# Output projection and second feed-forward matrix of a fused block in products of 512 columns instead of 256

## The chip, the cores and the metric

One core of a Trainium2 chip runs the whole program. Its engines are TensorE (PE; a matmul is a MATMUL and a LDWEIGHTS of its stationary operand, shown as PEld), VectorE (DVE), ScalarE (ACT), GpSimd (POOL) and SyncE (SP), which issues most transfers. The metric is device time in microseconds: 2568.1 us, the median of three runs (2564.01 to 2571.09).

## The reference

A block of a hybrid model on 1024 tokens of width 1024, in float32. Cut to what the change touches:

```python
h = _rms(x, norm_mix_g)
p_nsa, p_rwkv, p_gdn, p_gate = split(h @ w_in)
o_a, o_b, o_c = _nsa(p_nsa), _rwkv7(p_rwkv), _gdn(p_gdn)          # 1024 x 512 each
gate = sigmoid(p_gate.reshape(1024, 3, 1024))
merged = gate[:, 0] * (o_a @ w_branch[0]) + gate[:, 1] * (o_b @ w_branch[1]) + gate[:, 2] * (o_c @ w_branch[2])
x = x + merged @ w_out                                            # 1024 x 1024
h = _rms(x, norm_ffn_g)
x = x + square(relu(h @ w_ff1)) @ w_ff2                           # 1024 x 4096, 4096 x 1024
```

## The kernel before

**Split products.** Every large product is made of three: each float32 operand is split into a rounded part (`hi`, type float32r) and a rest (`lo`), and hi·hi, hi·lo and lo·hi are summed in PSUM. A weight tile therefore goes through `load_w` (L242): SP transfers it into `wraw`, ACT casts it into `whi` (L253), and the rest `wraw - whi` goes into `wlo` (L258), which VectorE and GpSimd share as the argument `div` says. With `(1, 2)` VectorE takes the first half of the tile's row blocks and GpSimd the second, with `(0, 1)` GpSimd takes all. `TRAW` is the number of `wraw` buffers, `TBUF` that of `whi` and of `wlo`, for the first and the second tail.

**The tail.** `tail(hf, ...)` computes everything behind the three mixers for 512 tokens; `hf` is 0 or 1, so it runs twice. Its stages:

1. Branch products. For each of three branches, four tiles `or` of the mixer's output (128 x 512 each) are loaded and split into `oh` and `ol` (`OBUF` buffers each). Then for each of eight column blocks: load a weight tile of 512 x 128, load the gate tile `gin` (ACT makes a tanh of it in place), 12 matmuls of 512 columns, and VectorE multiplies the sum in PSUM by the gate (L1470). From the second branch on GpSimd adds this to `ms` (L1472). The third branch's results are split into `mh` and `ml`.
2. Output projection, by `accum` (L1430). The stationary operand is a 128 x 128 piece of `mh` or `ml` (128 tokens), the moving one a piece of the weight tile. One call takes 256 output columns and all eight row blocks (two weight tiles of 512 x 256); for each of four token blocks `st` it makes 24 matmuls of 256 columns and one add to `acc` (L1442), a tile that already holds `x`. Four calls cover the 1024 columns.
3. Norm (`norm_T`): the rows of `acc` are normalised, transposed and split into `h2h` and `h2l`.
4. Feed-forward, in eight groups of four row blocks of 128. `up` makes one block: two weight tiles of 512 x 128, 24 matmuls of 512 columns with the weight tile as stationary operand, then relu (ACT), square (VectorE) and the split into `fh` and `fl`. After the four (in the first group five) `up` of a group, four calls of `accum` bring the group's share of the second matrix into `acc`: each has one weight tile of 512 x 256, four token blocks, 12 matmuls of 256 columns and an add. So a group is 96 matmuls of 512 columns and 192 of 256.
5. Four writes of `acc` to `out` (L1519).

**What sets the order.** The first tail is a job that is stepped through beside the second half of the sparse attention (`nsa`, whose PSUM tiles are called `mps`, the tails' `fps`): `run` (L166) takes a piece of the tail whenever a share of PE's modelled time is owed to it, a piece being what lies between two `yield`. When the attention is done the rest of the first tail follows, then the second tail. The tile framework's scheduler, with a model of the times, then orders the instructions of each engine, and within an engine they run in that order. While the attention runs, two PSUM buffers serve the tail; afterwards there are six (`pst`, L1569).

## Time and profile before

| | |
|---|---|
| median of three runs | 2568.1 us (2564.01 to 2571.09) |
| the profiled execution | 2570.32 us, span 2568.6 us |
| mean granted PE clock | 0.964 |
| PE busy | 2414.0 us, 94% |
| DVE, ACT, POOL busy | 1488.7, 1044.3, 989.9 us |
| DMA | 217.05 MB, mean 84 GB/s |

The span runs from the first to the last instruction; the 1.7 us around it belong to the execution's time. Matmuls are pipelined, so the busy times of neighbours overlap: what a matmul occupies PE for is the distance from its start to the next one's start. Rows of several like instructions are merged (`x4`), with one duration for all. A few matmul records are missing from a trace. In the brackets of a timeline row stands the engine's idle time before it and who ended it.

### The profile page before, as it was taken

How to read it: one execution, taken by the hardware profiler on the slowest of the kernel's cores; microseconds unless marked ns; L12 is line 12 of the kernel's file. 1: busy time of each engine (PE TensorE's matmuls, PEld its weight loads, DVE VectorE, ACT ScalarE, POOL GpSimd, SP SyncE). 2: the span in 40 equal slices, each digit the busy share in tenths (PEclk: the TensorE clock that was granted, in tenths of full speed). 3: DMA queues.
4: the chain of work that ended last, by engine and by line, in shares of the span. 5: the costliest groups of instructions: out<-in, count | busy, mean ns of one | idle time of the engine just before them, and what ended most of it. 6: DMA issues, size and time to landing. Idle time of an engine off the chain costs nothing.

```text
span 2568.6 us, 41137 instructions
## 1 busy us (share of the span) xinstructions
PE 2414.0 (94%) x15509; PEld 2013.4 (78%) x15509; DVE 1488.7 (58%) x3325; ACT 1044.3 (41%) x2085; POOL 989.9 (39%) x975
## 2 busy tenths in 40 slices
PE   7989899999898999989999999899999999999999
PEld 4767676777777777777887778788888878899988
DVE  4587877673576666223557787764454444545444
ACT  5333423332343333225667675753322333423232
POOL 4444433333322121234446675343332345223332
PEclk9889889999999999999999999899999999999999
DMA  4222222222223122362214331025322354223233
GB/s 135 66 54 66 57 52 66 70 55 79 67 66 83 40 54 76 114 137 76 61 50 141 101 102 37 20 72 154 95 91 86 104 160 132 78 87 107 83 104 102
DMA packets 340214, 217.05 MB, mean 84 GB/s; under 512 B 78486, under 2 KB 314144, under 8 KB 340016
## 3 DMA queue, kind: packets, MB, share of 16 engines
q1 hardware_dynamic: 329152, 195.63, 27.2%
q10 hardware_dynamic: 9792, 17.83, 1.9%
q8 instruction: 122, 2.00, 0.3%
q0 software_dynamic: 1072, 0.96, 0.2%
q14 instruction: 76, 0.62, 0.1%
HBM read 178.16 MB, written 36.22 MB: 83 GB/s over the span
## 4 chain that ended last, share of the span: by engine, by line
PE 71%; DVE 15%; DMA 6%; ACT 4%; issue 2%; POOL 1%; SPq 0%; ACTq 0%; DVEq 0%; POOLq 0%
PE fps L96 53%; PE mps L96 15%; PE mps L100 3%; DVE inv_p L335 2%; DVE inv_u L337 1%; DMA gin<-gates 1%; DVE BK L549 1%; DVE gacc L881 1%; DMA cw<-in_nsa_cmp_w_dram 1%; DMA lb<-inv 1%; ACT P L1348 1%; DMA inv<-LT 1%; DVE ast L1343 1%; DVE PL L1391 1%; DVE AG L536 1%
## 5 line engine op out<-in xcount | busy, mean ns | idle before, releaser
L258 POOL TENSOR_TENSOR wlo<-wraw,whi 128x512 fp32r<-128x512 f32 (+2 forms) x408 | 528.6, 1297 | 940.1 <-ACT whi L253 907.4
L253 ACT CAST whi<-wraw 128x512 fp32r<-128x512 f32 (+1 forms) x408 | 286.2, 703 | 699.5 <-PE fps L96 612.0
L96 PE MATMUL fps<-hTh,whi 128*128 128x512 f32 x1024 | 448.7, 440 | 6.7 <-ACT rraw L423 3.5
L96 PE MATMUL fps<-hTh,wlo 128*128 128x512 f32 x1024 | 416.4, 411 | 3.4 <-POOL wlo L258 3.4
L96 PE MATMUL fps<-hTl,whi 128*128 128x512 f32 x1024 | 418.1, 410 | 0.0
L96 PE MATMUL fps<-wlo,fh 128*128 128x256 f32 x1024 | 266.6, 284 | 7.0 <-DVE wlo L258 7.0
L96 PE MATMUL fps<-whi,fl 128*128 128x256 f32 x1024 | 266.7, 283 | 0.0
L96 PE MATMUL fps<-whi,fh 128*128 128x256 f32 x1024 | 266.0, 284 | 0.6
L258 DVE TENSOR_TENSOR wlo<-wraw,whi 128x256 fp32r<-128x256 f32 (+1 forms) x207 | 142.2, 690 | 180.2 <-ACT whi L253 180.1
L96 PEld LDWEIGHTS fps<-hTh,wlo 128*128 128x128 f32 x1024 | 200.7, 196 | 50.8 <-POOL wlo L258 5.2
L96 PEld LDWEIGHTS fps<-hTh,whi 128*128 128x128 f32 x1024 | 201.4, 197 | 49.0 <-ACT whi L253 3.8
L96 PEld LDWEIGHTS fps<-hTl,whi 128*128 128x128 f32 x1024 | 202.4, 198 | 32.5
L1442 DVE TENSOR_TENSOR acc<-fps,acc 128x256 f32<-128x256 f32 x288 | 118.6, 422 | 178.5 <-PE fps L96 178.1
L96 PE MATMUL fps<-h2h,whi 128*128 128x512 f32 x512 | 200.1, 391 | 0.9 <-DVE h2l L290 0.9
L96 PE MATMUL fps<-h2h,wlo 128*128 128x512 f32 x512 | 200.0, 391 | 0.2 <-DVE wlo L258 0.2
L96 PE MATMUL fps<-h2l,whi 128*128 128x512 f32 x512 | 199.8, 390 | 0.0
L1362 POOL TENSOR_SCALAR P<-P,ast 128x64 f32<-128x64 f32 (+5 forms) x128 | 138.6, 1100 | 144.7 <-DVE ast L1355 112.6
L96 PEld LDWEIGHTS fps<-wlo,fh 128*128 128x128 f32 x1024 | 186.3, 192 | 8.8 <-DVE wlo L258 8.4
L96 PEld LDWEIGHTS fps<-whi,fh 128*128 128x128 f32 x1024 | 186.9, 192 | 3.8 <-ACT whi L253 2.2
L96 PEld LDWEIGHTS fps<-whi,fl 128*128 128x128 f32 x1024 | 187.4, 192 | 0.1
L1348 ACT ACTIVATE P<-mps,ast 128x128 f32<-128x128 f32 (+4 forms) x256 | 125.1, 494 | 80.5 <-DVE ast L1346 47.3
L1343 DVE TENSOR_REDUCE ast<-mps 128x1 f32<-128x128 f32 (+4 forms) x256 | 109.0, 441 | 49.5 <-PE mps L96 47.3
(465 smaller groups left out, 4946.4 us busy)
## 6 DMA issues: line engine op xcount, KB each, us to landing
wraw<-in_w_in_dram SPq DMA_DIRECT2D x152, 256.0 KB, 2.9
wraw<-in_w_ff_dram SPq DMA_DIRECT2D x128, 256.0 KB, 2.9
wraw<-in_w_ff_dram SPq DMA_DIRECT2D x64, 512.0 KB, 3.4
gates<-fst ACTq DMA_DIRECT2D x48, 256.0 KB, 2.0
wraw<-in_w_branch_dram SPq DMA_DIRECT2D x48, 256.0 KB, 3.0
gin<-gates SPq DMA_DIRECT2D x48, 256.0 KB, 3.0
wraw<-in_w_out_dram SPq DMA_DIRECT2D x16, 512.0 KB, 3.6
nsa_in<-fst ACTq DMA_DIRECT2D x20, 256.0 KB, 2.1
```

The costliest lines, as they stand in the source:

```text
L96: return self.note(self.nc.tensor.matmul(out, lhsT=lhsT, rhs=rhs, **kw))
L100: return self.note(self.nc.tensor.transpose(out, x, ident))
L253: nc.scalar.copy(hi, raw)
L258: eng.tensor_tensor(out=lo[:, x], in0=raw[:, x], in1=hi[:, x].bitcast(F32), op=OP.subtract)
L335: nc.vector.tensor_tensor(out=v, in0=lt[:n, s, None, s + 1:].to_broadcast([n, w, w]), in1=u[:n, s + 1:, s + 1:].rearrange("p t c -> p c t" ...
L337: nc.vector.tensor_reduce(out=u[:n, s, s + 1:], in_=v, axis=AX, op=OP.add)
L536: stt(out=ag[o, :, :, h], in0=ch2(sg)[o, :, c2], scalar=-1.0, in1=ch2(kk)[o, :, c2], op0=OP.mult, op1=OP.mult)
L549: tt(out=BK[HH[h], :, :, 1 - (x ^ h)], in0=ch2(t)[HH[h]], in1=ch2(WI)[HH[h]], op=OP.mult)
L1343: nc.vector.tensor_reduce(out=(mx if i == 0 else mx2)[:, b:b + 1], in_=ps[:, :n], axis=AX, op=OP.max, negate=True)
L1348: nc.scalar.activation(out=Pt[:, c:c + n], in_=tiles[i][:, :n], func=AF.Exp, bias=mx[:, b:b + 1], accum_out=(sm if i == 0 else sm2)[:, b:b ...
L1362: eng.tensor_scalar(out=Pt[:, c:c + n], in0=Pt[:, c:c + n], scalar1=r[:, b:b + 1], scalar2=None, op0=OP.mult)
L1442: tt(out=acc[:, st, c0:c0 + 256], in0=ps, in1=acc[:, st, c0:c0 + 256], op=OP.add)
```

## The change

`accum` takes 512 output columns and four row blocks in one call, instead of 256 columns and all row blocks (eight in the output projection). Its weight tiles are two row blocks by 512 columns, two of them to a call; they have as many bytes as the old ones of four by 256. A token block's sum is 12 matmuls of 512 columns and one add of 512. The output projection calls it for two column halves and two halves of the row blocks, a feed-forward group for two column halves. `yield` now stands behind each three matmuls of 512 columns instead of each six of 256.

The buffers: `whi` and `wlo` have three in the first tail and four in the second, not two; `oh` and `ol` four, not five; `or` and `gin`, which had two each, share three; `fh` and `fl` five in the first tail, not six.

```diff
--- before.py
+++ after.py
@@ -42,11 +42,12 @@
 TDIV = ((0, 1), (1, 2))
 FDIV = (0, 1)
 TRAW = (2, 2)
-TBUF = (2, 2)
+TBUF = (3, 4)
 FSPLIT = (1, 1)
 FRAW = 2
 FBUF = 2
-OBUF = 5
+OBUF = 4
+FBUFS = (5, 6)
 POOLB = (0, 2)
 KVBUF = 2
 SABUF = 5
@@ -1418,8 +1419,8 @@
 
         div = lambda: TDIV[hf] if self.tasks else TDIV[1]
 
-        def load(src, cols):
-            return self.load_w(src, 4, cols, wp, wbufs, TRAW[hf], div())
+        def load(src, kt, cols):
+            return self.load_w(src, kt, cols, wp, wbufs, TRAW[hf], div())
 
         with pool("tacc") as ap, pool("tw") as wp:
             acc = ap.tile([P, 4, D], F32, name="acc")
@@ -1427,19 +1428,18 @@
                 nc.sync.dma_start(out=acc[:, st], in_=a["x"][0, T.start + st * P:T.start + (st + 1) * P, :])
 
 
-            def accum(lhs, w_rows, kt, c0):
-                ws = [load(w_rows[j * 512:(j + 1) * 512, c0:c0 + 256], 256) for j in range(kt // 4)]
+            def accum(lhs, w_rows, k0, c0):
+                ws = [load(w_rows[(k0 + j) * P:(k0 + j + 2) * P, c0:c0 + 512], 2, 512) for j in (0, 2)]
                 for st in range(4):
                     m = slice(st * P, (st + 1) * P)
-                    ps = psum()[:, 0:256]
-                    for k in range(kt):
-                        (wh, wl), j = ws[k // 4], k % 4
-                        self.te.matmul(ps, lhsT=lhs[0](k)[:, m], rhs=wh[:, j, :], start=(k == 0), stop=False)
-                        self.te.matmul(ps, lhsT=lhs[0](k)[:, m], rhs=wl[:, j, :], start=False, stop=False)
-                        self.te.matmul(ps, lhsT=lhs[1](k)[:, m], rhs=wh[:, j, :], start=False, stop=(k == kt - 1))
-                        if k % 2:
-                            yield
-                    tt(out=acc[:, st, c0:c0 + 256], in0=ps, in1=acc[:, st, c0:c0 + 256], op=OP.add)
+                    ps = psum()
+                    for k in range(4):
+                        (wh, wl), j = ws[k // 2], k % 2
+                        self.te.matmul(ps, lhsT=lhs[0](k0 + k)[:, m], rhs=wh[:, j, :], start=(k == 0), stop=False)
+                        self.te.matmul(ps, lhsT=lhs[0](k0 + k)[:, m], rhs=wl[:, j, :], start=False, stop=False)
+                        self.te.matmul(ps, lhsT=lhs[1](k0 + k)[:, m], rhs=wh[:, j, :], start=False, stop=(k == 3))
+                        yield
+                    tt(out=acc[:, st, c0:c0 + 512], in0=ps, in1=acc[:, st, c0:c0 + 512], op=OP.add)
 
             with pool("tm") as mp:
                 mt = lambda n, dt=F32R, bufs=KT: mp.tile([P, 512], dt, name=n, tag="m" + n[-1], bufs=bufs)
@@ -1448,7 +1448,7 @@
                     for b in range(3):
                         oh, ol = [], []
                         for k in range(4):
-                            raw = op.tile([P, 512], F32, name="or", tag="or", bufs=2)
+                            raw = op.tile([P, 512], F32, name="or", tag="gin", bufs=3)
                             nc.sync.dma_start(out=raw, in_=self.o_spill["abc"[b]][k, :, T])
                             hi = op.tile([P, 512], F32R, name="oh", tag="oh", bufs=OBUF)
                             lo = op.tile([P, 512], F32R, name="ol", tag="ol", bufs=OBUF)
@@ -1456,8 +1456,8 @@
                             oh.append(hi)
                             ol.append(lo)
                         for dt in range(KT):
-                            wh, wl = load(a["w_branch"][0, b][:, dt * P:(dt + 1) * P], P)
-                            g = op.tile([P, 512], F32, name="gin", tag="gin", bufs=2)
+                            wh, wl = load(a["w_branch"][0, b][:, dt * P:(dt + 1) * P], 4, P)
+                            g = op.tile([P, 512], F32, name="gin", tag="gin", bufs=3)
                             nc.sync.dma_start(out=g, in_=self.gates[b * KT + dt, :, T])
                             nc.scalar.activation(out=g, in_=g, func=AF.Tanh, scale=0.5)
                             ps = psum()
@@ -1476,8 +1476,9 @@
                                 nc.scalar.activation(out=mh[dt], in_=m[dt], func=AF.Copy, scale=0.5)
                                 stt(out=ml[dt], in0=m[dt], scalar=0.5, in1=mh[dt].bitcast(F32), op0=OP.mult, op1=OP.subtract)
                 lhs = tuple((lambda k, t=t: t[k]) for t in (mh, ml))
-                for c0 in range(0, D, 256):
-                    yield from accum(lhs, a["w_out"][0], KT, c0)
+                for c0 in range(0, D, 512):
+                    for k0 in range(0, KT, 4):
+                        yield from accum(lhs, a["w_out"][0], k0, c0)
 
             with pool("th") as hp:
                 h2 = tuple(hp.tile([P, KT, 512], F32R, name=n) for n in ("h2h", "h2l"))
@@ -1490,15 +1491,15 @@
                     def up(ft):
                         ps = psum()
                         for kh in range(2):
-                            wh, wl = load(a["w_ff1"][0][kh * 512:kh * 512 + 512, ft * P:(ft + 1) * P], P)
+                            wh, wl = load(a["w_ff1"][0][kh * 512:kh * 512 + 512, ft * P:(ft + 1) * P], 4, P)
                             for j in range(4):
                                 k = kh * 4 + j
                                 self.te.matmul(ps, lhsT=wh[:, j], rhs=h2[0][:, k], start=(k == 0), stop=False)
                                 self.te.matmul(ps, lhsT=wh[:, j], rhs=h2[1][:, k], start=False, stop=False)
                                 self.te.matmul(ps, lhsT=wl[:, j], rhs=h2[0][:, k], start=False, stop=(k == KT - 1))
                                 yield
-                        hi = fp.tile([P, 512], F32R, name="fh", tag="fh", bufs=6)
-                        lo = fp.tile([P, 512], F32R, name="fl", tag="fl", bufs=6)
+                        hi = fp.tile([P, 512], F32R, name="fh", tag="fh", bufs=FBUFS[hf])
+                        lo = fp.tile([P, 512], F32R, name="fl", tag="fl", bufs=FBUFS[hf])
                         r = fp.tile([P, 512], F32, name="fr", tag="fr", bufs=2)
                         nc.scalar.activation(out=r, in_=ps, func=AF.Relu)
                         tt(out=r, in0=r, in1=r, op=OP.mult)
@@ -1511,8 +1512,8 @@
                             yield from up(ft)
                         now, fs = fs[:G], fs[G:]
                         lhs = (lambda k: now[k][0], lambda k: now[k][1])
-                        for c0 in range(0, D, 256):
-                            yield from accum(lhs, a["w_ff2"][0][g * P:(g + G) * P, :], G, c0)
+                        for c0 in range(0, D, 512):
+                            yield from accum(lhs, a["w_ff2"][0][g * P:(g + G) * P, :], 0, c0)
             self.summed = True
             yield
             for st in range(4):
```

On PE, the first tail's feed-forward behind the attention, before: the end of a group's first two `accum` calls and the start of the third. `whi_18043` and `whi_18169` are the weight tiles of the first and third call, `fps_18174` to `fps_18216` the four token blocks' sums of the third.

```order
L96 MATMUL fps_18048<-whi_18043,fh_17988 128x256
L96 MATMUL fps_18048<-wlo_18044,fh_17988 128x256
L96 MATMUL fps_18048<-whi_18043,fl_17989 128x256
L96 MATMUL fps_18174<-whi_18169,fh_17598 128x256
L96 MATMUL fps_18188<-whi_18169,fh_17598 128x256
L96 MATMUL fps_18202<-whi_18169,fh_17598 128x256
L96 MATMUL fps_18216<-whi_18169,fh_17598 128x256
L96 MATMUL fps_18188<-wlo_18170,fh_17598 128x256
```

Now, the same group's end of the first call and the second half of the second. `whi_17627` and `whi_17634` are the first call's two weight tiles, `whi_17704` is the second tile of the second call; `fps_17639` is the first call's first sum, `fps_17765` the next `up`.

```order
L97 MATMUL fps_17639<-whi_17627,fl_17481 128x512
L97 MATMUL fps_17639<-whi_17634,fh_17526 128x512
L97 MATMUL fps_17639<-wlo_17635,fh_17526 128x512
L97 MATMUL fps_17639<-whi_17634,fl_17527 128x512
L97 MATMUL fps_17639<-whi_17634,fh_17572 128x512
L97 MATMUL fps_17639<-wlo_17635,fh_17572 128x512
L97 MATMUL fps_17639<-whi_17634,fl_17573 128x512
L97 MATMUL fps_17709<-whi_17704,fh_17526 128x512
L97 MATMUL fps_17737<-whi_17704,fh_17526 128x512
L97 MATMUL fps_17723<-whi_17704,fh_17526 128x512
L97 MATMUL fps_17751<-whi_17704,fh_17526 128x512
L97 MATMUL fps_17765<-h2h_15819,whi_17768 128x512
```

A call's first sum is put off until the others of its call are done, in both orders. Before, the third weight tile is wanted directly behind the last product with the first one; now the fourth tile is wanted seven products behind the last product with the first.

On SP, the joint of the two tails, before: `w_ff` is the first tail's last group, `out_dram` its result, `gin` and `w_branch` belong to the second tail.

```order
L245 DMA wraw<-in_w_ff_dram 128x4x128 x6
L245 DMA wraw<-in_w_ff_dram 128x4x256 x4
L1519 DMA out_dram<-acc 128x1024
L1461 DMA gin<-gates 128x512
L245 DMA wraw<-in_w_branch_dram 128x4x128
L1519 DMA out_dram<-acc 128x1024
L1461 DMA gin<-gates 128x512
L245 DMA wraw<-in_w_branch_dram 128x4x128
L1519 DMA out_dram<-acc 128x1024
L1461 DMA gin<-gates 128x512
```

And now:

```order
L246 DMA wraw<-in_w_ff_dram 128x4x128 x6
L246 DMA wraw<-in_w_ff_dram 128x2x512 x4
L1452 DMA or<-o_a 128x512 x3
L1520 DMA out_dram<-acc 128x1024 x4
L1452 DMA or<-o_a 128x512
L1461 DMA gin<-gates 128x512 x5
L246 DMA wraw<-in_w_branch_dram 128x4x128
L1461 DMA gin<-gates 128x512
L246 DMA wraw<-in_w_branch_dram 128x4x128
L1461 DMA gin<-gates 128x512 x2
```

The first branch's tiles `or` have moved from well before the last group to either side of the four writes, which stand together, and five gate tiles follow before the next weight tile.

## Rows read from the trace of the kernel before

**Rows 1.** The page: busy time by engine; chain by line, shares of the span.
```profile
PE 2414.0 (94%) x15509; PEld 2013.4 (78%) x15509; DVE 1488.7 (58%) x3325; ACT 1044.3 (41%) x2085; POOL 989.9 (39%) x975
...
PE fps L96 53%; PE mps L96 15%; PE mps L100 3%; DVE inv_p L335 2%; DVE inv_u L337 1%; DMA gin<-gates 1%; DVE BK L549 1%; DVE gacc L881 1%; DMA cw<-in_nsa_cmp_w_dram 1%; DMA lb<-inv 1%; ACT P L1348 1%; DMA inv<-LT 1%; DVE ast L1343 1%; DVE PL L1391 1%; DVE AG L536 1%
```

**Rows 2.** Chain of waits, 1500 us to the end: start us, us, what.
```profile
1784.58 1.59 DVE wlo L258
...
2087.28 3.40 DMA gin<-gates
...
2205.17 359.31 PE fps L96 x2304
```

**Rows 3.** Stretches: us; PE, PEld, DVE, ACT, POOL busy (instructions); PE clock; DMA share; GB/s.
```profile
1400.00:1500.00 100.00, 94.17 (x550) 76.02 (x548) 75.48 (x166) 67.37 (x175) 71.25 (x57) 1.00 0.31 95
2205.00:2568.60 363.60, 359.46 (x2306) 328.50 (x2304) 172.95 (x292) 107.77 (x162) 113.83 (x94) 1.00 0.31 96
```

**Rows 4.** PE by time, second tail: start us, us, line, out<-in.
```profile
2232.55 0.64 PE L96 MATMUL fps<-whi,fh 128*128 128x256 f32 x4
...
2255.58 0.40 PE L96 MATMUL fps<-h2h,whi 128*128 128x512 f32 x1
...
2277.36 0.64 PE L96 MATMUL fps<-whi,fh 128*128 128x256 f32 x4
```

**Rows 5.** All engines by time, first tail: a group's bounds, and inside.
```profile
1819.18 0.64 PE L96 MATMUL fps<-whi,fh 128*128 128x256 f32 x4
...
1829.86 2.09 ACT L253 CAST whi<-wraw 128x1024 fp32r<-128x1024 f32 x2 [5.56 <-PE fps L96]
...
1830.96 0.74 PE L96 MATMUL fps<-whi,fh 128*128 128x256 f32 x4
1830.99 2.97 POOL L258 TENSOR_TENSOR wlo<-wraw,whi 128x512 fp32r<-128x512 f32 x2 [7.89 <-ACT whi L253]
1831.24 3.27 DVE L258 TENSOR_TENSOR wlo<-wraw,whi 128x512 fp32r<-128x512 f32 x2
1832.87 0.61 PE L96 MATMUL fps<-wlo,fh 128*128 128x256 f32 x3 [1.16 <-DVE wlo L258]
...
1865.82 0.64 PE L96 MATMUL fps<-whi,fh 128*128 128x256 f32 x4
```

**Rows 6.** Groups by shape, 2100 to 2560 us: busy us, mean ns.
```profile
L258 POOL TENSOR_TENSOR wlo<-wraw,whi 128x512 fp32r<-128x512 f32 x40 | 70.9, 1775 | 112.7 <-ACT whi L253 112.6
L1442 DVE TENSOR_TENSOR acc<-fps,acc 128x256 f32<-128x256 f32 x140 | 58.0, 422 | 90.1 <-PE fps L96 90.1
L253 ACT CAST whi<-wraw 128x1024 fp32r<-128x1024 f32 x40 | 41.9, 1048 | 90.4 <-PE fps L96 83.7 <-DMA wraw<-in_w_ff_dram 4.6 <-DMA wraw<-in_w_out_dram 2.1
L258 DVE TENSOR_TENSOR wlo<-wraw,whi 128x512 fp32r<-128x512 f32 x40 | 30.4, 759 | 37.5 <-ACT whi L253 37.5
L1472 POOL TENSOR_TENSOR ms<-ms,gin 128x512 f32<-128x512 f32 x16 | 24.1, 1507 | 5.8 <-DVE gin L1470 2.9 <-PE fps L96 2.6
L1470 DVE SCALAR_TENSOR_TENSOR gin<-gin,fps 128x512 f32<-128x512 f32 x14 | 9.6, 683 | 13.1 <-ACT gin L1462 11.4 <-PE fps L96 1.7
L1462 ACT ACTIVATE gin<-gin 128x512 f32<-128x512 f32 x14 | 8.8, 631 | 16.5 <-DMA gin<-gates 14.9 <-DVE wlo L258 1.6
```

**Rows 7.** DMA issues, from the page: KB each, median us to landing.
```profile
wraw<-in_w_ff_dram SPq DMA_DIRECT2D x64, 512.0 KB, 3.4
gin<-gates SPq DMA_DIRECT2D x48, 256.0 KB, 3.0
```

**Rows 8.** PE by time: last group of the first tail, first product of w_out.
```profile
2046.91 0.64 PE L96 MATMUL fps<-whi,fh 128*128 128x256 f32 x4
...
2146.88 0.66 PE L96 MATMUL fps<-whi,mh 128*128 128x256 f32 x4
```

**Rows 9.** Waits of PE beside the attention, 1383 to 1742 us: total, times.
```profile
PE mps L96 <- ACT P L1348: 7.5, 9, 1.7
PE mps L96 <- DVE PL L1391: 5.5, 5, 2.3
```

## The prediction

> **What bounds the kernel now.** I read the page's first and fourth parts, then the chain of waits in order of time, then the busy table by stretch, and last TensorE's own timeline where the chain lies on it. PE is busy for 94% of the span, and its products at L96 are 53% (the tails' and projections', `fps`) and 15% (`mps`) of the chain [rows 1]. In order of time the last 800 us are nearly all PE: in the first tail long pieces of it, parted by six pieces of 1.59 us of DVE writing `wlo`; one piece of 359.31 us in the second tail; and only around 2087 us a handful of waits for the gate tiles `gin` [rows 2]. The granted clock is 1.00 there and in the stretch where the first tail runs beside the attention, and PE is busy for 94 of 100 us even in that one [rows 3]. So a product that takes less of PE's time shortens the kernel nearly one for one, and everything else counts only where PE waits for it.
>
> **What a product costs.** Busy time is no price: matmuls overlap, so I take the distance between starts. In the second tail a group is 96 products of 512 columns (`up`) and 192 of 256 (`accum`). The 192 run from 2232.55 to 2255.58, 23.03 us, 0.1199 each; the 96 from 2255.58 to 2277.36, 21.78 us, 0.2269 each [rows 4]. Two of 256 cost 0.2399, one of 512 costs 0.2269: 13.0 ns less for the same columns. (256 more columns cost 107.0 ns, so 12.9 ns of either are a fixed part; 107.0 ns is one column a cycle at 2.4 GHz, the level of the granted clock of 1.00.) The changed kernel has half as many weight loads and half as many such parts. Products of 256 columns per tail: `accum` for the output projection 4 x 4 x 24 = 384, for the second feed-forward matrix 8 x 192 = 1536; both tails 3840, which become 1920 of 512. 1920 x 13.0 ns = 25.0 us. Of it 10.0 are in the second tail's groups (768 pairs), 2.5 in its output projection (192), 9.2 in the first tail's groups behind the attention (709), and 3.3 beside the attention (251).
>
> The Trainium skill (TensorE: Matmul & The Clock Gate, "Back-to-back issue gap") speaks against this: there a warm product of N columns takes N / 2.4 GHz plus 2.5 ns, so a pair would save 2.5 ns and the term would be 4.8 us. The rows have 13 ns at both widths, so the trace does not agree, and I go by it.
>
> **The wait inside the first tail's groups.** A group of the first tail lasts longer than one of the second: 1819.18 to 1865.82 is 46.64 us against 2232.55 to 2277.36, 44.81: 1.83 us more, with the same instructions [rows 4, 5]. Where it goes: at 1830.96 PE has issued four products with the third load's `whi` and stands until 1832.87; ACT's cast of that load began at 1829.86, when the buffer came free, GpSimd began its half at 1830.99, VectorE its half at 1831.24 behind an add to `acc`, and beside GpSimd it needed 1.59 us [rows 2, 5] where its mean for that tile is 0.76 [rows 6]. With two buffers the third load can't be split before an earlier one is used up. The chain shows this six times, so 6 x 1.83 = 11.0 us hang on it.
>
> In the changed order the place looks like this, counted from the end of the last `up` of a group with PE at 0.2269 a product. The sum that starts first is set aside after one product and finished late, so the first load's last reader is the 66th product. It starts at 65 x 0.2269 = 14.7 us and takes 0.40 [rows 4]; the fourth load waits for that, its cast takes 1.05 [rows 6], and `whi` is there at 16.2. PE needs it as the 73rd product, at 16.3. VectorE's half (0.76 to 1.59) is needed six products later, at 17.7, GpSimd's (1.78) twenty later, at 20.9. What is late next is thus the cast, by 0 to 0.3 us with the hand-overs. The first three loads are ahead: their transfers take 3.4 us [rows 7], two may be under way, and a step of 48 products now lasts 10.9 us instead of 5.8. I take 0.3 a group: 11.0 - 1.8 = 9.2 us gained. Bounds: all 11.0, or nothing if the old loss stays. The second tail has no such loss now, and with four buffers each load of a step has its own; nothing there.
>
> **The second tail's branch products.** From the last 256-column group of the first tail (2046.91) to the first product of the output projection (2146.88) are 99.97 us [rows 4, 8]. They hold 192 products of 256 and 3 x 8 x 12 = 288 of 512: 23.03 + 65.35 = 88.4 us. 11.6 us are lost, and the chain shows mostly transfers of `gin`. A `gin` buffer is held for the transfer 3.0 [rows 7], the tanh and the product (0.63 and 0.68) and, from the second branch on, GpSimd's add, 1.51 [rows 6]: 5.8 us. Two buffers give one product column block each 2.9 us, PE wants one each 2.72 (12 x 0.2269); three give 1.9. Against that, the raw tiles `or` now take turns in the same three buffers and `oh`/`ol` have four, not five: at each change of branch the third raw tile waits for the last `gin` of the branch before, 0.68 + 1.51 after its last product, then come 3.0 of transfer [rows 7] and some 0.6 each of cast and split (the tanh of that shape takes 0.63 [rows 6]), 6.4 in all, while PE has 24 products (5.4 us) on the first two: 1 to 3 us lost, twice. At the joint of the tails the four writes of `out` now stand ahead of all gate loads in SP's queue, and of the fourth `or`. PE has 36 products (8.2 us) before it needs that tile, which comes 0.68 (add) + 3.0 + 1.2 = 4.9 us, four issues and some hand-overs after the last product: 0 to 1.5 us. The seventh weight tile stands behind five gate loads, the last of which waits for the second product block: 0 to 1.5. Together 2 to 9 us where 11.6 are lost now. I take the upper end, 2.5 gained, as the ring of three has more takers; bounds from 9.6 gained to 10 lost, for no row shows this ring.
>
> **Small things.** An add to `acc` of 512 columns isn't in the trace; the nearest row is the product out of PSUM of that shape, 0.68 us against 0.42 for the add of 256 [rows 6]; below it can't fall under 0.42, above not beyond two of those. Three of these end a stretch that PE waits for (the norm of each tail, the last write): 3 x 0.26 = 0.8 us lost. The others lie beside products. The output projection's adds double in columns (16 x 0.26 = 4.2 us more of VectorE in each tail). In the second tail PE covers them. In the first they meet the attention, where PE stood for 13 us behind ACT's `P` and VectorE's `PL` [rows 9].
>
> **Beside the attention.** The order places the attention's last products deeper in the tail's work (behind the first group and into the next four `up`, no longer two thirds into the first group), in smaller pieces. No row of the kernel before shows what this order waits for. Below: the pieces fill the 13 us that PE stood, and a little more where it was free; 15 gained. Above: the finer alternation doubles the 13 and VectorE's 4.2 come on top; 20 lost, rounded up. PE is busy there for 94 of 100 us, so I take 0, beyond the 3.3 us of the rate.
>
> **Sum.** 25.0 + 9.2 + 2.5 - 0.8 = 35.9 us less. The profiled execution took 2570.3 us (span 2568.6); 2534.4. The median shown is 2568.1, 2.2 lower; so 2532. Its own range, with each term near its value: 2520 to 2546.
>
> **Rivals.** (a) The fixed part doesn't halve: the 512-column rows have another stationary operand (a weight tile, not `fh`), and if with `fh` the fixed part grew with the columns, nothing would come of the 25.0: 9.2 + 2.5 - 0.8 = 10.9 less, 2557. Against it, `up` and `accum` show the same 13 ns in the same stretch [rows 4]. With the 2.5 ns of the Trainium skill's page for a pair it would be 2552. (b) The alternation beside the attention costs the 20 us bounded above: 2552. For it speaks that the attention's chain goes through VectorE and ACT; against it the 94%. (c) It gains 15: 2517. (d) Slower than before: a step now needs two whole loads before it can end, and the second becomes the bound. If the second load's transfer too waited for the buffer, 3.4 + 1.05 + 1.80 = 6.3 us would stand against 2.7 us of work (12 products), 3.6 lost in each of the first tail's 20 steps, 72 us: 2604. It decides from 36 / 20 = 1.8 us a step. Two raw tiles ahead and four open sums in the order speak against it. That nothing changes would need two of these together.
>
> **Chances.** Forecast 0.63, (a) 0.06, (b) 0.15, (c) 0.10, (d) 0.06. 2508 to 2558 leaves out (d) and little else. What a measurement can tell from no change is 0.3%, 7.7 us: (b) lies 16 us below the median and (a) 11, with some 0.04 of both inside the bound. Faster 0.90, same 0.04, slower 0.06.
>
> **What would show it.** Right: in the second tail 192 products of 512 in 43.6 us a group without idle time; in the first, groups of 43.6 to 44.2 with no 1.6 us wait for `wlo`; 1920 pairs' worth of LDWEIGHTS gone; branch products of the second tail ending 65.4 + 9 us after the last group. Wrong: products of 512 with `fh` as stationary operand more than 0.235 apart; a wait for `whi` or `wlo` once a step; PE idle beyond 40 us beside the attention.

## The result, and the profile after

The changed kernel takes 2528.95 us (median of 4 runs, 2524.64 to 2535.23), the one before, run beside it, 2566.06 (4 runs, 2561.18 to 2571.09): ratio 0.9857, 95% interval 0.9827 to 0.9887, 37.1 us less. The forecast was 2532. The profiled execution took 2527.64 us, span 2525.9, mean granted PE clock 0.965.

The page of the changed kernel, busy time by engine, and two groups of costly instructions (busy us, mean ns). It answers to [rows 1, 6]:

```profile
PE 2377.5 (94%) x13589; PEld 1907.6 (76%) x13589; DVE 1472.0 (58%) x3197; ACT 1043.1 (41%) x2083; POOL 986.8 (39%) x975
...
L97 PE MATMUL fps<-whi,fl 128*128 128x512 f32 x512 | 191.0, 389 | 0.0
...
L1442 DVE TENSOR_TENSOR acc<-fps,acc 128x512 f32<-128x512 f32 x160 | 106.7, 686 | 101.4 <-PE fps L97 101.0
```

The 1920 matmuls and as many weight loads are gone (15509 to 13589), the share of PE is the same 94%, and the add of 512 columns, which no row of before had, takes 0.69 us (0.68 had been taken).

PE by time in the second tail (start us, us, what): first product of a group's `accum`, first `up`, next group. It answers to [rows 4]:

```profile
2200.12 0.39 PE L97 MATMUL fps<-whi,fh 128*128 128x512 f32 x1
...
2221.88 0.39 PE L97 MATMUL fps<-h2h,whi 128*128 128x512 f32 x1
...
2243.64 0.39 PE L97 MATMUL fps<-whi,fh 128*128 128x512 f32 x1
```

96 products of `accum` take 21.76 us, 96 of `up` 21.76: 0.2267 each, whichever the stationary operand. A group is 43.52 us, where it was 44.81.

The same in the first tail, two groups' starts, with the start of the second group and of the last one; it answers to [rows 5, 8]:

```profile
1755.56 0.62 PE L97 MATMUL fps<-whi,fh 128*128 128x512 f32 x2
...
1842.60 1.07 PE L97 MATMUL fps<-whi,fh 128*128 128x512 f32 x4
...
1886.12 1.07 PE L97 MATMUL fps<-whi,fh 128*128 128x512 f32 x4
...
2011.24 1.07 PE L97 MATMUL fps<-whi,fh 128*128 128x512 f32 x4
```

Here too a group is 43.52 us, to the hundredth what it is in the second tail. It was 46.64: the wait for `wlo` is gone.

The chain of waits from 1500 us on, its long pieces (start us, us, what), against [rows 2]:

```profile
1741.21 291.29 PE fps L97 x1284
...
2053.01 4.94 DMA wraw<-in_w_branch_dram
...
2061.97 4.19 DMA or<-o_b
2067.33 3.52 DMA gin<-gates
...
2085.51 3.85 DMA or<-o_c
...
2172.74 348.51 PE fps L97 x1536
```

What was PE parted by six pieces of `wlo` is one piece of 291 us. In the second tail's branch stage, though, the chain, which ran mostly through `gin`, now runs through the weight tiles `wraw` and the raw tiles `or`. PE at the change to the third branch, and its first product of the output projection:

```profile
2090.05 2.07 PE L97 MATMUL fps<-oh,whi 128*128 128x512 f32 x4 [5.29 <-ACT oh L254]
...
2114.85 1.20 PE L97 MATMUL fps<-whi,mh 128*128 128x512 f32 x4
```

and the windows around it (us; busy by engine; PE clock; DMA share; GB/s):

```profile
2085.00:2090.00 5.00, 0.00 (x0) 0.00 (x0) 2.56 (x4) 2.49 (x4) 4.26 (x5) 0.80 0.78 230
2090.00:2095.00 5.00, 4.95 (x12) 3.90 (x13) 2.50 (x4) 2.11 (x4) 3.42 (x5) 0.51 0.81 243
2095.00:2100.00 5.00, 5.00 (x24) 4.13 (x23) 0.60 (x2) 2.10 (x4) 1.53 (x2) 1.00 0.42 138
```

PE stands for 5.29 us; afterwards it gets 12 products through in 5 us, not the 24 of the next window, at a granted clock of 0.51. The wait thus costs some 2.3 us more than it shows. The stage had such a fall before the change, too, behind a wait of 1.78 us for `whi`; in 3.4 us at half the clock it lost about 1.7:

```profile
2123.30:2126.70 3.40, 3.40 (x10) 2.66 (x9) 0.43 (x1) 1.25 (x2) 2.55 (x4) 0.50 0.66 205
```

**Where the time went, stage by stage.** The two profiled executions are 42.7 us apart in span, the medians 37.1. Part of that stands ahead of the change: the last product of the gates, in code that both share, came 9.6 us later in the execution of before:

```profile
1356.25 0.39 PE L96 MATMUL fps<-hTh,wlo 128*128 128x512 f32 x1
```

and in that of after:

```profile
1346.61 0.39 PE L97 MATMUL fps<-hTh,wlo 128*128 128x512 f32 x1
```

So each stage is taken between starts of PE's products, from that landmark on (us; ff2 is the second feed-forward matrix):

| stage | before | after | measured | forecast |
|---|---|---|---|---|
| gates to second ff2 group (beside attention) | 416.2 | 409.0 | -7.2 | -3.5 |
| second to last ff2 group of the first tail | 274.5 | 255.7 | -18.8 | -16.7 |
| last ff2 group to w_out of the second tail | 100.0 | 103.6 | +3.6 | -3.8 |
| w_out to first up of the second tail | 58.3 | 57.9 | -0.4 | -2.2 |
| first up to the end | 363.4 | 353.2 | -10.3 | -9.7 |
| sum | | | -33.1 | -35.9 |

The forecast column splits the terms of the prediction by the same cuts: 16.7 is six groups' rate (7.5) and the wait (9.2); 3.8 the branch stage's 2.5 and the rate of the first tail's last group (1.3), which lies in that stretch; 3.5 the rest of the first tail's rate, less its norm's add. One execution of each stands behind a row of this table, so a few us of a stage that waits on transfers may be the execution's own: in the seven traces of this document with the first tail of after, the first stretch takes 408.5 to 411.5. The landmark itself, in code that all kernels here share, lies between 1342.1 and 1356.3 us over all twelve traces of this document.

### The profile page after: what moved, and what is told of

Read it like the earlier page. It is cut to its first block, busy times and chain, and to the rows that moved or that the text cites. A ratio compares the mean times of both kernels' runs of the same rounds, so it can differ in the third digit from the quotient of the medians.

```text
span 2525.9 us, 37184 instructions
## 1 busy us (share of the span) xinstructions
PE 2377.5 (94%) x13589; PEld 1907.6 (76%) x13589; DVE 1472.0 (58%) x3197; ACT 1043.1 (41%) x2083; POOL 986.8 (39%) x975
## 4 chain that ended last, share of the span: by engine, by line
PE 72%; DVE 13%; DMA 6%; ACT 4%; issue 2%; POOL 2%; SPq 0%; ACTq 0%; POOLq 0%; DVEq 0%
PE fps L97 53%; PE mps L97 15%; PE mps L101 3%; DVE inv_p L336 2%; DVE inv_u L338 1%; DVE gacc L882 1%; DVE BK L550 1%; DMA cw<-in_nsa_cmp_w_dram 1%; POOL wlo L259 1%; DMA lb<-inv 1%; ACT P L1349 1%; ACT whi L254 1%; DMA wraw<-in_w_branch_dram 1%; DVE ast L1344 1%; DMA gin<-gates 1%
## 5 line engine op out<-in xcount | busy, mean ns | idle before, releaser
L259 DVE TENSOR_TENSOR wlo<-wraw,whi 128x256 fp32r<-128x256 f32 (+1 forms) x207 | 129.7, 629 | 232.5 <-ACT whi L254 227.0
L97 PE MATMUL fps<-whi,fl 128*128 128x512 f32 x512 | 191.0, 389 | 0.0
L97 PE MATMUL fps<-whi,fh 128*128 128x512 f32 x512 | 189.9, 391 | 0.0
L97 PE MATMUL fps<-wlo,fh 128*128 128x512 f32 x512 | 189.0, 389 | 0.0
L1442 DVE TENSOR_TENSOR acc<-fps,acc 128x512 f32<-128x512 f32 x160 | 106.7, 686 | 101.4 <-PE fps L97 101.0
L1392 DVE TENSOR_TENSOR PL<-mps,PH 128x512 fp32r<-128x512 f32 (+2 forms) x168 | 103.3, 619 | 47.7 <-ACT PH L1391 47.0
L1391 ACT CAST PH<-mps 128x512 fp32r<-128x512 f32 (+2 forms) x168 | 88.1, 533 | 63.5 <-PE mps L101 58.1
L97 PEld LDWEIGHTS fps<-h2h,whi 128*128 128x128 f32 x512 | 96.2, 188 | 21.5 <-DVE h2l L291 1.8
```

Source lines behind the costliest of these rows:

```text
L97: return self.note(self.nc.tensor.matmul(out, lhsT=lhsT, rhs=rhs, **kw))
L259: eng.tensor_tensor(out=lo[:, x], in0=raw[:, x], in1=hi[:, x].bitcast(F32), op=OP.subtract)
L1391: nc.scalar.copy(PH[:n, x0:x1], ps[:n, x0:x1])
L1392: tt(out=PL[:n, x0:x1], in0=ps[:n, x0:x1], in1=PH[:n, x0:x1].bitcast(F32), op=OP.subtract)
L1442: tt(out=acc[:, st, c0:c0 + 512], in0=ps, in1=acc[:, st, c0:c0 + 512], op=OP.add)
```

## Experiments

Where two kernels differ in several buffers, the names are: **ring** for `or` and `gin` sharing three buffers (with `oh`, `ol` at four, and five `fh`, `fl` in the first tail), **weight buffers** for three and four `whi`/`wlo`, not two.

**The width alone, taken back.**

```diff
-for k in range(4):
-    matmul(ps, ..., rhs=wh[:, j, :]) ...
+for x, k in ((slice(i * 256, i * 256 + 256), k) for i in range(2) for k in range(4)):
+    matmul(ps[:, x], ..., rhs=wh[:, j, x]) ...
```

> The changed kernel, with each sum of 512 columns made of two of 256, one after the other in the halves of the same PSUM tile; weight tiles, buffers and adds of 512 columns stay. If a product has a fixed part of 13 ns whatever its width, a group of the second tail takes 44.8 us instead of the 43.5 measured with 512 columns, and the whole about 25 us more, near 2554. Rival: the gain is not in the number of products but in the tiles and adds; then a group stays at 43.5 and the whole near 2529.

Measured: 2594.86 us (2589.15 to 2597.69), ratio to before 1.0119, interval 1.0097 to 1.0142. Two groups' starts in its second tail:

```profile
2296.94 0.28 PE L97 MATMUL fps<-whi,fh 128*128 128x256 f32 x1
...
2341.76 0.28 PE L97 MATMUL fps<-whi,fh 128*128 128x256 f32 x1
```

44.82 us, what before had, and 1.30 more than after: the price per pair (96 x 13 ns = 1.25) is confirmed where nothing waits. The total is 40 us above what that price explains: its first tail's groups took 46.3 to 49.1 us, with waits for `whi` and `wlo`, and its branch stage 115.4, with PE waiting 6.64 us for `oh` once and 5.51 once more. Both weight tiles of a call are now needed twice in turn and held till the last half, which would fit the groups; why the branch stage lost as well is not shown. So this kernel can't price the width as a whole, only in the second tail's groups.

**Buffers alone, at 256 columns.** Before, with ring and weight buffers as in after:

```diff
-TBUF = (2, 2)
+TBUF = (3, 4)
-OBUF = 5
+OBUF = 4; FBUFS = (5, 6)
-raw = op.tile(..., tag="or", bufs=2);  g = op.tile(..., tag="gin", bufs=2)
+raw = op.tile(..., tag="gin", bufs=3); g = op.tile(..., tag="gin", bufs=3)
```

> The kernel before with all buffer numbers of the change (three and four weight buffers, the ring of three for or and gin, four oh/ol, five fh/fl) but products and weight tiles of 256 columns as they were. If buffers alone take the wait for the third load away, the groups of the first tail go from 46.6 to 44.8 us (11 us in all), those of the second stay at 44.8, and the branch products of the second tail lose 5 us as they do in the changed kernel: near 2560. Rival: the wait goes only with the longer step of 512 columns; then groups stay at 46.6 us and the time is 2566 to 2571.

Measured: 2562.8 us (2554.38 to 2568.51), ratio 1.0001, interval 0.9987 to 1.0015. Two groups of its first tail:

```profile
1843.99 0.64 PE L97 MATMUL fps<-whi,fh 128*128 128x256 f32 x4
...
1888.82 0.64 PE L97 MATMUL fps<-whi,fh 128*128 128x256 f32 x4
```

44.83 us: the third weight buffer removes the wait for `wlo` at the old width (the next run has the ring without it, and the wait). But its branch stage took 111.4 us, with PE waiting at the changes of branch, and what the one gives the other takes:

```profile
2047.30 2.07 PE L97 MATMUL fps<-oh,whi 128*128 128x512 f32 x4 [5.31 <-ACT oh L254]
...
2103.53 2.07 PE L97 MATMUL fps<-oh,whi 128*128 128x512 f32 x4 [5.61 <-ACT oh L254]
```

**The ring alone, at 256 columns.** The same with `TBUF = (2, 2)`.

> The kernel before, with the ring of three for or and gin, four oh/ol and five fh/fl of the change, but two weight buffers and 256 columns. With all buffers of the change and 256 columns the stretch from the last group of the first tail to the output projection took 111.4 us instead of 100.0. If the ring does that, it takes 108 to 113 here as well, groups stay at 46.6, and the whole is 2572 to 2578. Rival: it is the four weight buffers, with which the branch products are no longer placed beside the last group; then the stretch stays at 98 to 103 and the whole at 2562 to 2568.

Measured: 2572.66 us (2565.5 to 2579.08), ratio 1.0027, interval 1.0009 to 1.0045. Groups of the first tail 46.64, as before; gates to second group 425.5 (before: 416.2), branch stage 104.2 (before: 100.0). The ring alone costs time, in both tails; the stage came out below what was expected for it.

**The width with two weight buffers.**

```diff
-TBUF = (3, 4)
+TBUF = (2, 2)
```

> The changed kernel with two weight buffers in both tails instead of three and four. If the third buffer is what keeps a step of two loads from standing, each step now waits for the cast and the split of its second tile behind the last step's end, 0.6 to 1.6 us: a group (two steps, eight loads for up) takes 45 to 47 us instead of 43.5, in both tails, and the whole 2550 to 2580. Rival: the scheduler's order with several open sums hides it: groups stay at 43.5 to 44, the whole near 2530.

Measured: 2538.85 us (2536.73 to 2549.56), ratio 0.9894, interval 0.9861 to 0.9928; between the two expectations. From its gates to its second group, and two groups further on:

```profile
1343.24 0.39 PE L97 MATMUL fps<-hTh,wlo 128*128 128x512 f32 x1
...
1769.72 1.07 PE L97 MATMUL fps<-whi,fh 128*128 128x512 f32 x4
...
1813.24 1.07 PE L97 MATMUL fps<-whi,fh 128*128 128x512 f32 x4
```

The groups are 43.52 us with two buffers too; the theory that they would wait has fallen. The first stretch is 426.5 us, 17.5 more than in after. So the third weight buffer earns its time beside the attention; behind it, the change of `accum` makes the wait go with two buffers as well. It is not that a weight tile serves PE longer: 24 products of 0.2267 are 5.4 us, the 48 of 0.1199 before were 5.8. The order is another. ACT's cast of a group's third load (the second call's first tile; the group starts at 1856.76), and PE's first product with it:

```profile
1863.12 1.05 ACT L254 CAST whi<-wraw 128x1024 fp32r<-128x1024 f32 x1 [2.22 <-PE fps L97]
...
1867.64 0.62 PE L97 MATMUL fps<-whi,fh 128*128 128x512 f32 x2
```

The buffer came free 4.5 us before PE needed the tile; in the kernel before, the cast of a group's third load began at 1829.86, and PE was there 1.1 us later [rows 5].

**The ring taken back in the second tail.** After, with `or` and `gin` in two buffers of their own there, and five `oh`, `ol`:

```diff
-raw = op.tile(..., tag="gin", bufs=3)
+raw = op.tile(..., tag=("gin", "or")[hf], bufs=(3, 2)[hf])
-g = op.tile(..., tag="gin", bufs=3)
+g = op.tile(..., tag="gin", bufs=(3, 2)[hf])
```

> The changed kernel, with the second tail's or and gin in two buffers each and five oh/ol, as before the change; the first tail unchanged. From the last group of the first tail to the first product of the output projection the changed kernel takes 103.6 us, of which 16.5 are lost. If the ring of three is what loses (11.6 were lost before), this goes to about 98.7 and the whole to 2524. Rival: what loses is the order at the joint, where the branch products no longer run beside the last group; then it stays at 102 to 104 and the whole at 2529.

Measured: 2524.35 us (2519.66 to 2531.88), ratio 0.985, interval 0.9825 to 0.9875. Branch stage 100.87 us (after: 103.61). The long wait for `oh` is gone, short ones for `whi` (0.5 to 2.4 us, 5.7 in all) stand in its place. This lies between the two expectations. The ring explains 2.7 of the 3.6 us that the stage lost, as far as one trace of each can say; what the order at the joint adds is not parted from the rest.

**More buffers there.** Second tail: `or` four of its own, `gin` four, `oh` and `ol` eight, four raw weight buffers.

```diff
-TRAW = (2, 2); OBUF = 4
+TRAW = (2, 4); OBUF = (4, 8)
-raw = op.tile(..., tag="gin", bufs=3);                g = op.tile(..., bufs=3)
+raw = op.tile(..., tag=("gin", "or")[hf], bufs=(3, 4)[hf]); g = op.tile(..., bufs=(3, 4)[hf])
```

> The changed kernel, with more buffers in the second tail alone: gin four, or three of its own, oh/ol eight, wraw four. If the branch products wait for transfers that could have been under way earlier, most of the 16.5 us lost there go and the 3 us lost in the output projection: 103.6 becomes 90 to 95, and the whole 2515 to 2522. Rival: the transfers themselves are the bound in that stretch, and the time stays at 2526 to 2530.

Measured: 2522.35 us (2521.01 to 2525.13), ratio 0.9841, interval 0.9822 to 0.9859. Branch stage 91.5 us, of which the products are 87.1 (384 x 0.2269); but from w_out to the first `up` 62.2 (after: 57.9). PE now comes to the output projection's weights sooner than they do: it waits 4.5 us for their casts and splits (after: 1.9), and the mean granted clock of the stretch is 0.92 (after: 0.97).

> The version with larger branch buffers in the second tail, with the second tail's weights in five split buffers, not four, and three raw buffers, not four. Theory (its output projection, 62.2 us to the first up product against 57.9 in the kernel after, waits because four split buffers are all held by the branch stage's last sums): 58 to 59 us there, the branch stage stays at 91 to 93, the run is 2517 to 2520 us. Rival (the waits there are for the queue of transfers and splits, not for a buffer): 61 to 63 us there, and 2521 to 2525 us.

This kernel has five split and three raw weight buffers in the second tail (`TRAW = (2, 3)`, `TBUF = (3, 5)`). Measured: 2521.23 us (2517.89 to 2523.34), ratio 0.983, interval 0.9798 to 0.9861; branch stage 88.6, w_out to `up` 62.8. The split buffers were not what w_out waited for; the rival holds. (Six of them beside four raw ones, the version first meant to settle this, gave no time: it needs 48 KB a partition for the branch stage's tiles, where 42 are left.)

> The version with larger branch buffers in the second tail, with two raw weight buffers there, not four. Theory (raw buffers let the branch and w_out weights be loaded early; two hold them to the splits): branch stage back to 95 to 100 us, run 2527 to 2532 us. Rival (the branch stage is freed by the oh, ol and gate buffers alone): 91 to 93 us there, run 2520 to 2525 us.

With `TRAW = (2, 2)`. Measured: 2522.02 us (2516.1 to 2528.04), ratio 0.9842, interval 0.9803 to 0.9881; branch stage 92.3, w_out to `up` 59.8. Raw weight buffers aren't needed; `or`, `gin`, `oh` and `ol` free the stage. Its clock in that stage:

```profile
2009.00:2101.00 92.00, 89.09 (x386) 71.44 (x384) 43.48 (x70) 38.17 (x64) 51.69 (x48) 1.00 0.60 196
```

Of the 11 to 15 us that these three gain in the branch stage, w_out gives back 2 to 5. Their medians lie 6.6 to 7.7 us below that of after, the intervals of the ratios overlap with its own: that they beat it is read from the stages, not from the ratios.

**What a product costs at other widths.** After, with the second tail's `accum` in four products of 128 columns:

```diff
-for k in range(4):
+for x, k in ((slice(i * w, i * w + w), k) for w in ((512, 128)[hf],) for i in range(512 // w) for k in range(4)):
```

> The changed kernel, with the sums of the second tail's accum made of four products of 128 columns each instead of one of 512; the first tail, tiles, buffers and adds unchanged. If the fixed part of 13 ns holds at any width, a product of 128 takes 53 + 13 = 66 ns and a group of the second tail 384 x 0.066 + 21.8 = 47.2 us. Rival: the distance can't go below what a weight load takes, and 256 columns just cover it: then 128 columns cost as much as 256, 0.12, and a group takes 21.8 + 46.1 = 67.9 us.

Measured (one run): 2849.19 us. Two groups' starts:

```profile
2380.74 0.22 PE L97 MATMUL fps<-whi,fh 128*128 128x128 f32 x1
...
2445.44 0.22 PE L97 MATMUL fps<-whi,fh 128*128 128x128 f32 x1
```

64.70 us: less the `up`'s 21.76, 42.9 for 384 products, 0.112 each. That is close to one of 256 (0.120) and far from the 0.067 of 128 columns plus 13 ns: the fixed part does not carry down to 128. The windows of the output projection and of one group's `accum`:

```profile
2116.00:2280.00 164.00, 161.56 (x757) 161.18 (x756) 27.38 (x33) 12.90 (x18) 17.60 (x13) 0.50 0.09 26
2316.00:2358.00 42.00, 42.00 (x378) 41.96 (x377) 10.47 (x14) 4.53 (x7) 5.18 (x4) 1.00 0.13 38
```

PE's weight loads (the second figure) are busy for 41.96 of 42 us. That would fit a limit by the loads, one per product, but doesn't show it: in the kernel before, in a stretch of products of 256 columns, they are just as full, and there the distance follows the columns.

```profile
2233.00:2255.00 22.00, 22.00 (x186) 22.00 (x185) 10.82 (x21) 4.44 (x6) 6.37 (x4) 1.00 0.27 84
```

The first window holds most of the rest of the loss (w_out to the first `up` took 176.3 us, not 57.9): behind a wait of 1.86 us the granted clock fell to 0.50 and stayed there for 164 us of products of 128 columns, now 0.2133 apart. It happened once more in the last group: behind a wait of 1.66 us the clock fell, and products of 128 columns ran at 0.50 to the end. The two waits, and the last stretch:

```profile
2114.91 0.33 PE L97 MATMUL fps<-wlo,mh 128*128 128x128 f32 x1 [1.86 <-DVE wlo L259]
...
2770.83 0.33 PE L97 MATMUL fps<-whi,fh 128*128 128x128 f32 x1 [1.66 <-ACT fh L254]
...
2775.00:2847.50 72.50, 67.62 (x317) 67.43 (x317) 5.53 (x8) 0.00 (x0) 0.00 (x0) 0.50 0.08 29
```

The same with 384 and then 128 columns (`slice(0, 384), slice(384, 512)`):

> The kernel after, with each sum of 512 columns of the second tail (w_out and second feed-forward matrix) made as 384 columns and then 128, so two products per pair in place of one. Products of 512 and of 256 advance 0.2269 and 0.1199 us here, those of 128 advanced 0.111. Theory (a fixed 13 ns above the columns' own time, for products of 256 columns and more): 384 advance 0.173 us, a group of the second tail is 21.8 + 96 x (0.173 + 0.112) = 49.1 us, and the run is near 2585 us. Rival (columns are taken in units of 256, a product of 128 costing nearly one of 256): 384 advance 0.227, a group is 54.3 us, and the run is near 2635 us. Of the clock in the output projection: it fell to 0.5 when that stage ran products of 128 alone; if the narrow products as such make it fall, it falls again to about 0.5 for that stage, which adds some 50 us; if not, it stays at 1.0 there.

Measured (one run): 2596.81 us; a group of the second tail 49.27, expected 49.1 or 54.3. Two groups' starts:

```profile
2321.01 0.33 PE L97 MATMUL fps<-whi,fh 128*128 128x384 f32 x1
...
2370.27 0.33 PE L97 MATMUL fps<-whi,fh 128*128 128x384 f32 x1
```

27.5 us for 96 pairs, 0.2866 each, less 0.112: 0.175, against 0.160 for the columns. The fixed part of 13 to 15 ns holds at 256, 384 and 512. In its output projection, where products of 384 and of 128 take turns, the clock stayed at 1.00, behind a wait of 1.49 us too:

```profile
2126.00:2160.00 34.00, 32.14 (x220) 31.49 (x221) 22.77 (x23) 10.82 (x13) 18.11 (x12) 1.00 0.35 113
```

## Why the prediction was right, and where it was off

The sum was 35.9 us; the medians show 37.1, the stages of the two traces 33.1. That it came so near is in part luck: the first tail gave 5.8 us more than forecast (table), the branch stage and the output projection 9.2 less, and 4 us of the medians' difference stand in no stage. By its steps:

- **The rate (25.0).** Right where nothing waits. In the second tail's groups 10.0 were forecast and 10.3 came; the width taken back costs 1.30 a group, with the buffers of before and of after. The 7.5 of the first tail's groups came as well. The 2.5 in the output projection and the 3.3 beside the attention can't be seen by themselves: the first went under in waits (below), and kernels that differ in width there take 410.9 and 409.0, or 425.5 and 426.5, apart by less than executions of the same code. Rival (a), that the fixed part doesn't halve, falls: products with `fh` and with a weight tile as stationary operand are 0.2267 apart alike. The Trainium skill (TensorE: Matmul & The Clock Gate, "Back-to-back issue gap") has 2.5 ns above the columns' time for an isolated product; the products here come in a stream with a weight load each and have 13 to 15 at three widths, so the figure doesn't carry over to them.
- **The wait in the first tail's groups (9.2 of 11.0).** Right, and the 0.3 a group that I left for the cast didn't come: groups of 43.52 in both tails. The cause was only half mine. I argued with the third buffer and the new order; two experiments show that either the third buffer (44.83 at 256 columns) or the new `accum` with its order (43.52 with two buffers) is enough.
- **The branch stage (2.5 gained).** Wrong in sign within its bounds (9.6 gained to 10 lost). The stage's products need 87.1 us now, so 16.5 of its 103.6 are lost, where 11.6 were: 4.9 lost, of which the rate of the last group hides 1.3 in the table. The branch products ended 81.9 us behind the last group, where the prediction had named 65.4 + 9 as a sign that it is right. The step that was mis-sized is the change of branch, put at 1 to 3 us lost twice. The first shows 2.2 us of wait; the second alone 5.29 and then 2.3 of half clock. The prediction let the third raw tile wait for the last `gin`, with 24 products on the first two to cover it. The trace shows all four late. PE's last product of the second branch, GpSimd's add of the third last `gin` tile, VectorE's products with the last two, and SP's issues of the third branch's raw tiles, in the kernel after:

```profile
2084.37 0.39 PE L97 MATMUL fps<-oh,wlo 128*128 128x512 f32 x1
```

```profile
2084.21 1.27 POOL L1472 TENSOR_TENSOR ms<-ms,gin 128x512 f32<-128x512 f32 x1
```

```profile
2085.93 0.69 DVE L1470 SCALAR_TENSOR_TENSOR gin<-gin,fps 128x512 f32<-128x512 f32 x1 [0.17 <-ACT gin L1462]
2087.43 0.69 DVE L1470 SCALAR_TENSOR_TENSOR gin<-gin,fps 128x512 f32<-128x512 f32 x1 [0.81 <-ACT gin L1462]
```

```profile
2085.51 0.32 SPq L1452 DMA_DIRECT2D or<-o_c  x1
2087.99 0.32 SPq L1452 DMA_DIRECT2D or<-o_c  x1
2090.52 1.19 SPq L1452 DMA_DIRECT2D or<-o_c  x2
```

  The gate tiles lag behind PE, whose finished sums wait in PSUM: VectorE takes the last two 1.6 and 3.1 us after PE's last product has started. In a ring of three the first raw tile needs the buffer of the third last `gin`, not a free one. GpSimd's add lets go of that at 2085.48, and the raw tile is issued 0.03 us later, 1.1 us after PE's last product, lands after 3.85, and is cast; none of PE's work is left to cover it. Then comes the clock, which I had at no cost; as the stage had lost 1.7 us to it before, too, it explains little of the difference. The ring taken back returns 2.7 us; own buffers for all return 11 to 15, and there the third branch's raw tiles are issued some 35 to 40 us ahead of need (the version with two raw weight buffers):

```profile
2033.29 0.80 SPq L1452 DMA_DIRECT2D or<-o_b  x2
...
2038.87 2.45 SPq L1452 DMA_DIRECT2D or<-o_c  x2
```

- **Output projection (2.2 with the norm).** Only 0.4 came: PE waits for the casts and splits of w_out's weights, 1.9 us in all, the longest 1.33, where before had no such wait; the chain has 4.47 and 4.87 us of `wraw<-in_w_out_dram` there. The prediction had no term for them.
- **Beside the attention (0, beyond the rate).** 7.2 less in that stretch where the rate and the norm give 3.5. By the experiments it isn't the width that does it: with ring and weight buffers it is 410.9 at 256 columns and 409.0 at 512, with the ring alone 425.5 and 426.5. A third weight buffer gives 14.5 to 17.5, the ring takes some 9. That the value of 0 came within 4 us is luck: two effects that I had not seen largely cancel. Rival (b), that the finer alternation costs 20, did not come: PE waits behind ACT's `P` and VectorE's `PL` fell [rows 9], while those behind ACT's `PH` rose from 1.1 to 3.0 us:

```profile
PE mps L97 <- ACT P L1349: 4.7, 8, 1.3
...
PE mps L97 <- DVE PL L1392: 2.7, 3, 2.1
```

- **Rival (d), two loads to a step.** The first tail's groups show no wait at all with three buffers, nor with two; it is refuted for this order. The kernel of two halves, in which both loads are held longer, shows what it looks like: waits for `whi` and `wlo` of up to 0.7 us and groups of up to 49 us.

Left open: why the unchanged code ahead of the gates took 9.6 us longer in one execution than in the other (the landmark's spread over the twelve traces does not follow the change); which of the ring's buffers costs the 9 us beside the attention, or whether it is the order that follows from them (the experiments change all at once); and what PE's weight loads have to do with the price of narrow products.

## What to carry to other kernels

Where TensorE is full, price a product by the distance of starts in a stretch without waits, at two widths, and ask what of it doesn't depend on the columns; wide products pay that part less often. A wait for a weight tile depends on how much of PE's work is left when a buffer comes free, so look at that point in the new order, too. A buffer taken from one place to pay for this shows up at the places where a stage changes, there with the wait and the lower clock after it: count who must let go of each buffer and what stands ahead of that instruction in its engine's queue. Take the sum stage by stage, since one stage here moved against its forecast, another gave little of it, and the total still came out right.

## What the runs showed of the hardware

- A product of 128 columns with a weight load of its own advances 0.112 us, hardly less than one of 256 (0.120), with weight loads busy for 41.96 of 42 us. At half the granted clock such products lie 0.2133 us apart. The Trainium skill (TensorE: Matmul & The Clock Gate, "LDWEIGHTS (loading the stationary operand)") takes P / 1.2 GHz for a load of P columns, 107 ns for the 128 here. The distance agrees with that within 5 ns at a granted clock of 1.00, not at 0.50. That the load is the limit is not shown: with products of 256 columns the loads are as busy (22.00 of 22.00 us).
- The granted clock fell to half (1.2 GHz) in a wait of 5.29 us in after, and was back at 1.00 within 5 us of products of 512 columns. In the run with products of 128 it fell behind waits of 1.86 and 1.66 us, and stayed at 0.50 for 164 us and for the last 72.5 us of such products, each a stretch without products of 512; in the same run 42 us of the same products kept 1.00 where products of 512 stood ahead of them.
